# Hybrid RWKV-7 block: the recurrence of four head pairs side by side, memory products ahead, the last gates after them

## The chip, the cores and the metric

The kernel runs on one core of one Trainium2 chip, as a single program. The metric is device time in microseconds of one execution, as the median of several; a profile is one further execution with the hardware profiler on. Engines are named as in the profile: PE (TensorE, products; PEld its weight loads), DVE (VectorE), ACT (ScalarE), POOL (GpSimd), SP (SyncE, which issues nearly all DMAs here).

## The reference, cut to what matters

One layer of a decoder with two parallel token mixers over 1024 positions of width 1024, then cross-attention to 256 memory tokens and a feed-forward of width 4096, all in float32.

```python
h = rms_norm(x, norm_mix)
p = h @ w_in                     # r, k, v, w/a/g-down | conv B, C, x | gate A | gate B
out_a = rwkv7_branch(...)        # 8 heads of 64; the state recurrence below
#   S_t = S_{t-1} diag(w_t) + (S_{t-1} a_t) b_t^T + v_t k_t^T ;  y_t = S_t r_t
#   y = layer_norm per head (y) + sum(r * k * r_k) * v      (the bonus)
out_b = short_conv_branch(cb, cc, cx, conv_w)              # B * conv3(C * x)
merged = sigmoid(ga + bg_a) * (out_a @ w_proj_a) + sigmoid(gb + bg_b) * (out_b @ w_proj_b)
x = x + merged @ w_out_mix
x = x + memory_cross_attention(rms_norm(x), rms_norm(mem), w_q, w_kv, w_xo)
x = x + relu(rms_norm(x) @ w_up)**2 @ w_down
return rms_norm(x)
```

## The kernel before

**Large products.** Each float32 product is made of three: both operands are split into a rounded high part and a low part, and high x high, high x low and low x high are accumulated in one PSUM bank. ACT makes the high part of a weight block and DVE the low part (`w_splits`, L515); raw weights of 512 KB come through two buffers `wr` (`w_loads`, L428, in the order of `wlist`). Tokens are in two blocks of 512 columns. A projection job (one block of 128 output columns, `gemm`, L822) is 2 x 8 x 3 = 48 products of 512 columns.

**The recurrence.** The 8 heads are 4 pairs `j`; a pair in one block `b` of 512 tokens is a *window*, with 8 chunks of 64 tokens. For each window `wkv_prepare` (L1267) loads r, k, v and the decays, forms the scaled operands T1 and BK, then the bonus (L1340), the values SV (L1358, through a PSUM bank and four DVE copies, L1370), the chunk products of BK with T1 (L1400) and the transposes of BK. `wkv_invert` (L1429) solves the triangular system of every chunk on POOL, in 31 steps, with round trips through HBM. `wkv_chain` (L1486) then runs the chunks of two windows together: products of T1 with the state SV, of SV with T1 for the output Y and of an identity with SV; a copy on ACT; products with the inverse XT and with QZ; four evacuations by ACT and DVE in turn, into SV; products with BKt; four evacuations into the next chunk's SV. All of these are small float32 products of 64 columns. `wkv_out` (L1554) normalizes Y and adds the bonus.

**The order of the work.** A planner written in the kernel (`Scheduler`, L42) fixes the order of every engine's instructions when the program is built. It keeps a clock for each engine from costs of its own (L68 to L119), and each stream of work is a generator that yields the time at which it may go on. `need(tile)` (L202) is the time at which a tile will have been written, plus 0.7 us; a write counts 0.21 us after its end for other engines (L168). The side streams (preparations, inversions, recurrence, loads) go first whenever their time has come, otherwise the main stream emits one more large product (`run`, L227). At run time nothing but the semaphores holds an engine up, and each engine takes its instructions in the order that was written. In `wkv_chain` the margins on `need` are +0.2 us (L1506, L1531).

Windows go in the order (pair, block) of `ORDER` (L1589); preparations come one after the other, inversions as well, and recurrences by twos. `held` and `LIVE_P` (L288, L1597) bound the SBUF tiles in use, `take_s` (L1253) the two PSUM banks `s`.

**Main stream.** `main` (L2111) runs the 43 projection jobs `PROJ` (L601; the last 16 are the gates gb and ga), then 8 jobs for the keys of the memory (`mem_k`, L1651, 24 products of 256 columns each), 4 for its values (`mem_v`, L1668, 256 columns), then 8 `merge` jobs (L1729) that need all outputs of the recurrence, and then the rest of the layer. Weights of the memory products are loaded up to four ahead (L431, L411). `mem_prep` (L1620) normalizes and transposes the memory tokens; `gate_loads` (L1717) brings the gates back from HBM for the merge, and begins when the projection jobs are over and the last recurrence is done. The evacuation of a "cc" job (L1204) scales by the square of the norm, held in a tile `Rq`; `lora_side` (L1111) writes its results through store buffers `st`.

Of the kernel before, what the change touches and what calls it, by code (L numbers as in the profile page):

```python
# [17 lines left out]
P = 128  # L18
D = 1024
# [242 lines left out]
def tile_hybrid_block(  # L262
# [130 lines left out]
    def w_wide(w, k0, c0):  # L393
        return [(w[k0:k0 + 512, c0:c0 + 256].rearrange("(k p) n -> p k n", p=P), 0, 4)], [P, 4, 256]
# [15 lines left out]
    def w_raw(i):  # L410
        n = 2 if i in quads else 1  # L411
        more = i >= first_quad and (i - first_quad) % 2 if i in quads else (i > first_quad or i in light) and i % 4 > 1
# [102 lines left out]
    def w_splits():  # L515
        for i in range(2, len(wlist)):
# [36 lines left out]
            parts = 4 if i - 1 in light or i in light else 1  # L553
# [52 lines left out]
    wlist += [w_cols(win, job_off(k, i), n=32 if (k, i) == ("gd", 1) else P) for k, i in PROJ]  # L606
    MIX = [("k", i) for i in range(8)] + [("v", i) for i in range(4)] + [("m", i) for i in range(8)]
    for k, n in MIX:
        if k != "m":
            light.update(range(len(wlist), len(wlist) + (2 if k == "v" else 1)))  # L610
        if k == "k":
            wlist.append(w_cols(w_kv[0], n * P))
        elif k == "v":
            wlist += [w_wide(w_kv[0], kh * 512, D + n * 256) for kh in range(2)]
        else:
            wlist.append(w_pair(w_proj_b[0], w_proj_a[0], n * P))
# [493 lines left out]

    def lora_side(name, parts, b, dst, fin):  # L1111
        yield until(("x", 1))
        for j in range(4):
# [41 lines left out]
    def proj_stream(t, b, o):  # L1155
# [48 lines left out]
        elif kind == "cc":  # L1204
            if "Rq" not in prevs:
                prevs["Rq"] = hold([P, NB, TB])
                for q in range(NB):
                    ACT.activation(prevs["Rq"][:, q], Rt[:, q], AF.Square)
            yield need(prevs["Rq"])
            z = sb("st", [P, TB])  # L1210
            DVE.tensor_tensor(z[:], o[:], prevs["Rq"][:, b], op=ALU.mult)
            yield need(z)
            prevs["cc", i, b] = z
            done.add(("cc", i, b))
        elif kind == "cx":
            if (i, b) == (3, 1):
                drop(1)
# [31 lines left out]
    open_s = {"n": 0}  # L1249
# [3 lines left out]
    def take_s():  # L1253

        yield lambda: open_s["n"] < BUFS["s"]
        open_s["n"] += 1
# [10 lines left out]
    def wkv_prepare(w):  # L1267
# [72 lines left out]
        POOL.tensor_tensor(ta, ta, k, op=ALU.mult)  # L1340
        yield max(pace("DVE"), need(ta_))
        DVE.scalar_tensor_tensor(sq, r, vc("rk", j), ta, op0=ALU.mult, op1=ALU.mult)
        bs = sb("P", [P, 2, TB], F32R)
        yield need(tm_, bs)
        split(bs[:, 0], bs[:, 1], sq)
        yield need(bs) + LATE
        yield from take_s()
        o = ps("s", [P, TB])
        yield need(o)
        mm(o[:], cv["bdo"][:], bs[:, 0], True, False)  # L1350
        mm(o[:], cv["bdo"][:], bs[:, 1], False, True)
        yield max(pace("DVE"), need(o))
        DVE.tensor_tensor(sw, o[:], v, op=ALU.mult)
        give_s()
        dma(d_bv[cs, blk(b)], sw, ("bv", j, b))


        SV = sb("P", [P, NCH, 2, C])  # L1358
        w["SV"] = SV
        yield from take_s()  # L1360
        o = ps("s", [P, 4, 2, C])
        yield need(o) + LATE
        for q in range(4):
            mm(o[:, q], v[:, q * P:(q + 1) * P], cv["cmat"][:].rearrange("p h k -> p (h k)"))
        yield need(o)
        for h in range(2):
            O = HALF[1 - h]
            for par in range(2):
                yield pace("DVE")
                DVE.tensor_copy(SV[O, par:NCH:2, h, :], o[HALF[par], :, h, :])  # L1370
        give_s()


        nt_ = sb("P", [P, TB])
        NT, QZ, XT = c3(nt_[:]), c3(v), c3(sw)
        w["vs"], w["NT"], w["QZ"], w["XT"] = vs_, NT, QZ, XT

        def evac_products(o, q, h):
# [7 lines left out]
            yield pace("DVE")  # L1386
            DVE.tensor_tensor(QZ[H, c4, :], o[H, :, C:2 * C], rows(msk[H, C:2 * C], 4), op=ALU.mult)
            give_s()

        for q in range(2):  # L1390
            yield need(T1[0], T1[1], BK) + 2 * LATE
            os_ = []
            for h in range(2):
                yield from take_s()
                o = ps("s", [P, 4, 2 * C])
                yield need(o) + LATE
                os_.append(o)
# [17 lines left out]
        w["BKt"] = BKt  # L1415

# [12 lines left out]
    def wkv_invert(w):  # L1429

        NT, XT, Lb = w["NT"], w["XT"], w["Lb"]
        zz = sb("ex", [P, 2, 8, 32])
# [18 lines left out]
        for g in range(4):  # L1451
            SP.dma_start(dz[:, :, g, :], Z[32 * g:32 * g + 32])
        for h in range(2):
# [4 lines left out]
        yield need(w["vs"])  # L1458
# [27 lines left out]
    def wkv_chain(ws):  # L1486

        b = ws[0]["b"]  # L1490
        HW = [(h, HALF[h], i, w) for i, w in enumerate(ws) for h in range(2)]
        for h, H, i, w in HW:
# [4 lines left out]
        Y = [ps(t, [P, NCH, C]) for t in "yc"]  # L1497
        yield need(*Y)
# [3 lines left out]

        for c in range(NCH):
# [6 lines left out]
            yield need(o)  # L1510
            for h, H, i, w in HW:
                acc_mm(w["T1"][h][:, c, 0:C], w["SV"][:, c, h, :], o[H, 0, i], i == 0, True)
            for h, H, i, w in HW:
                acc_mm(w["SV"][:, c, h, :], w["T1"][h][:, c, C:2 * C], Y[i][H, c], c == 0)
            if keep:
                for h, H, i, w in HW:
                    acc_mm(ident[:, H], w["SV"][:, c, h, :], o[H, 2, i], False)
            ws_ = sb("s2", [P, 2, C])
            ACT.activation(ws_[:], o[:, 0], AF.Copy)
            yield need(ws_)  # L1520
            for h, H, i, w in HW:
                acc_mm(w["XT"][H, c, :], ws_[H, i], o[H, 1, i], False, True)
            if c:
                for h, H, i, w in HW:
                    acc_mm(w["SV"][H, c - 1, h, :], w["QZ"][H, c - 1, :], Y[i][H, c - 1], False, True)
            for h, H, i, w in HW:
                if h == 0:
                    ACT.activation(w["SV"][H, c, h, :], o[H, 1, i], AF.Copy, scale=w["d2"][H, c:c + 1])
                else:
                    DVE.tensor_scalar(w["SV"][H, c, h, :], o[H, 1, i], w["d2"][H, c:c + 1], None, op0=ALU.mult)  # L1530
            yield need(*[w["SV"] for w in ws]) + 0.2  # L1531
            if keep:
                if last:
                    for w in ws:
                        state[w["j"]] = const([P, C], f"state{w['j']}")
                for h, H, i, w in HW:
                    acc_mm(w["BKt"][:, c, h, :], w["SV"][:, c, h, :], o[H, 2, i], False, True)
# [643 lines left out]
```

## Time and profile before

| | us |
|---|---|
| median of 3 runs (lowest, highest) | 1795.97 (1790.7, 1798.21) |
| profiled execution | 1803.41 |
| its span, first to last instruction | 1801.7 |
| PE busy | 1745.5 |
| DVE busy | 1081.4 |
| ACT busy | 698.2 |
| POOL busy | 519.6 |

The mean granted TensorE clock of this execution was 0.989. The profile names instructions by the tiles they write and read: `psc<-s,P` is a product into a bank `c` from tile `s`. All operations pass through one helper, so the line is L256 everywhere and one goes by tiles: `psg` are banks of the large products, `psc` and `psy` those of the recurrence, `pss` those of preparations and other side work; `wr`, `wh`, `wl` are raw, high and low weights. A row of the timeline has start, duration, engine, operation and count; in square brackets stands the idle time before it and what ended it. A row of the windows has the stretch, the busy time and count of PE, PEld, DVE, ACT and POOL, the granted clock (PEclk), the DMA share and GB/s. A row of the waits has who waited for whom: us in total, times, longest.

### The profile page before, as it was taken

What the parts mean: (1) busy time and instruction counts of PE and PEld (TensorE: products, weight loads), DVE (VectorE), ACT (ScalarE), POOL (GpSimd) and SP (SyncE); (2) the same over time, 40 slices, a digit from 0 to 9 for tenths busy, and PEclk for the clock granted to TensorE, in tenths of its full rate; (3) what the DMA queues carried; (4) which work ended last, traced back from release to release, by engine and by line L of the source; (5) the groups of instructions that cost most, each with busy time, mean ns of one, the idle gap of its engine ahead of it and who ended that gap; (6) DMA issues with size and microseconds to landing.
All of it is one profiled execution on the core that took longest, in us unless ns stands there. A gap on an engine that the chain in (4) does not pass through costs nothing. (4 is left out here: it accounts for less than half of the span.)

```text
span 1801.7 us, 26657 instructions
## 1 busy us (share of the span) xinstructions
PE 1745.5 (97%) x9914; PEld 1423.6 (79%) x9914; DVE 1081.4 (60%) x1694; ACT 698.2 (39%) x1233; POOL 519.6 (29%) x872
## 2 busy tenths in 40 slices
PE   7899999999999999999999999999999999999998
PEld 5687777877877778988888877778888887888887
DVE  4478666666665334555647666597776775645543
ACT  5524323123233434422324434364444454534532
POOL 3017643744653201001413334342322310000000
PEclk9999999999999999999999999999999999999999
DMA  6543532332433526645745667235545479755441
GB/s 211 203 125 96 163 109 74 91 101 68 129 112 107 175 89 228 210 152 191 243 143 160 207 203 253 97 114 169 176 157 170 135 244 339 251 207 192 152 125 51
DMA packets 303360, 289.19 MB, mean 161 GB/s; under 512 B 40745, under 2 KB 223135, under 8 KB 303231
## 3 DMA queue, kind: packets, MB, share of 16 engines
q1 hardware_dynamic: 302158, 286.97, 49.5%
q8 instruction: 78, 1.28, 0.3%
q10 hardware_dynamic: 1072, 0.53, 0.1%
q14 instruction: 52, 0.42, 0.1%
HBM read 193.06 MB, written 94.37 MB: 160 GB/s over the span
## 5 line engine op out<-in xcount | busy, mean ns | idle before, releaser
L256 PE MATMUL psg<-H,wh 128*128 128x512 f32 x1808 | 583.2, 400 | 1.0 <-ACT H L256 1.0
L256 PEld LDWEIGHTS psg<-H,wh 128*128 128x128 f32 x1808 | 338.9, 190 | 72.2 <-ACT H L256 1.4
L256 PE MATMUL psg<-P,wh 128*128 128x512 f32 (+1 forms) x1240 | 370.5, 380 | 2.7 <-DVE P L256 2.7
L256 PE MATMUL psg<-H,wl 128*128 128x512 f32 x888 | 356.6, 402 | 0.0
L256 PEld LDWEIGHTS psg<-P,wh 128*128 128x128 f32 x1240 | 228.0, 188 | 46.6 <-DVE P L256 4.4
L256 PE MATMUL psg<-P,wl 128*128 128x512 f32 (+1 forms) x620 | 235.4, 380 | 1.5 <-DVE wl L256 1.5
L256 ACT ACTIVATE wh<-wr 128x1024 fp32r<-128x1024 f32 (+2 forms) x155 | 127.1, 839 | 209.4 <-PE psg L256 143.1
L256 PEld LDWEIGHTS psg<-H,wl 128*128 128x128 f32 x888 | 168.7, 190 | 34.9 <-DVE wl L256 0.3
L256 DVE TENSOR_TENSOR wl<-wr,wh 128x1024 fp32r<-128x1024 f32 (+2 forms) x146 | 149.6, 1040 | 62.0 <-ACT wh L256 61.1
L256 ACT ACTIVATE P<-P 128x512 fp32r<-128x512 f32 (+3 forms) x246 | 148.1, 634 | 91.2 <-DVE P L256 55.6
L256 DVE TENSOR_TENSOR P<-P,P 128x512 fp32r<-128x512 f32 (+2 forms) x204 | 152.3, 782 | 14.1 <-ACT P L256 12.7
L256 POOL TENSOR_TENSOR sm<-sm,mhalf 128x8 f32<-128x8 f32 (+2 forms) x18 | 22.5, 1252 | 443.5 <-DVE sm L256 443.5
L256 PEld LDWEIGHTS psg<-P,wl 128*128 128x128 f32 x620 | 116.7, 188 | 22.7 <-DVE wl L256 1.9
L256 POOL TENSOR_TENSOR ex<-ex,P 128x60 f32<-128x60 f32 (+24 forms) x248 | 98.2, 396 | 101.3 <-DMA P<-dn 85.8
L256 POOL TENSOR_TENSOR ex<-ex 128x60 f32<-128x60 f32 (+24 forms) x248 | 95.7, 386 | 19.4
L256 PE MATMUL pss<-P,wh 128*128 128x512 f32 x304 | 93.9, 390 | 0.0
L256 DVE TENSOR_SCALAR P<-psc,sm 64x64 f32<-64x64 f32 x120 | 34.9, 291 | 83.7 <-ACT P L256 79.4
L256 ACT ACTIVATE P<-psc,sm 64x64 f32<-64x64 f32 (+1 forms) x128 | 42.4, 332 | 98.4 <-PE psc L256 54.8
L256 DVE TENSOR_TENSOR P<-psg,P 128x512 f32<-128x512 f32 x44 | 30.3, 689 | 78.4 <-PE psg L256 63.6
L256 PE MATMUL psc<-P,P 128*64 128x64 f32 (+2 forms) x816 | 65.0, 244 | 9.0 <-ACT st L256 7.9
L256 PEld LDWEIGHTS psc<-P,P 128*64 128x64 f32 (+2 forms) x816 | 44.8, 141 | 34.5 <-issue 11.6
L256 PE MATMUL psc<-P,wh 128*128 128x512 f32 x216 | 67.1, 391 | 1.7 <-DVE P L256 1.7
(698 smaller groups left out, 2837.3 us busy)
## 6 DMA issues: line engine op xcount, KB each, us to landing
P<-d_t SPq DMA_DIRECT2D x56, 512.0 KB
wr<-in_w_in_dram SPq DMA_DIRECT2D x40, 512.0 KB
d_t<-P SPq DMA_DIRECT2D x64, 256.0 KB
d_x<-P SPq DMA_DIRECT2D x48, 256.0 KB
P<-d_x SPq DMA_DIRECT2D x24, 512.0 KB
d_t<-st SPq DMA_DIRECT2D x48, 256.0 KB
d_tg<-st SPq DMA_DIRECT2D x32, 256.0 KB
P<-d_tg SPq DMA_DIRECT2D x16, 512.0 KB
```

Source lines behind the costliest of these rows:

```text
L256: return fn(*args, **kw)
```

## The change

- **Recurrence.** Windows go block by block, and `wkv_chain` takes the four pairs of a block together, with two banks `c` (two windows in each) per chunk and Y in a bank for two chunks, copied out every second chunk. Margins on `need` fall from +0.2 to -0.4 us (-0.1 for the first half of T1), the copies of T1's result come before Y and ident, and each of the steps with XT and BKt is done half by half.
- **Preparation.** The chunk products come right after the operands; bonus and values are a stream of their own. A window's preparation and inversion are one stream, and the next preparation begins when this one's operands are there; POOL's part of the inversion is still one window at a time.
- **Memory and gates.** Memory keys and values come before the last five gate jobs; the values are two jobs of 512 columns. Their weights keep to the two raw buffers. `mem_prep` takes one half of the memory tokens at a time.
- **Others.** Lora results go to held tiles. A "cc" job multiplies by the norm twice, the second time on POOL. `merge_loads` waits for the memory.

`finish(c)` does the products with QZ of the four windows and, after every second chunk, copies Y out, on ACT, one copy per window. The diff, cut to its core:

```diff
     def w_wide(w, k0, c0):
-        return [(w[k0:k0 + 512, c0:c0 + 256].rearrange("(k p) n -> p k n", p=P), 0, 4)], [P, 4, 256]
+        return [(w[k0:k0 + 256, c0:c0 + 512].rearrange("(k p) n -> p k n", p=P), 0, 2)], [P, 2, 512]
...
-                yield lambda: i < ws["split"] + (4 if i in light and "proj" in done else 2)
+                yield lambda: i < ws["split"] + 2
...
+    HEAD = len(PROJ) - 5
+    wlist += wcols[:HEAD]
+    wlist += [w_cols(w_kv[0], n * P) for n in range(KD)]
+    wlist += [w_wide(w_kv[0], kq * 256, D + n * 512) for n in range(2) for kq in range(4)]
+    light.update(range(HEAD, len(wlist)))
+    wlist += wcols[HEAD:]
...
-            z = sb("st", [P, TB])
-            fin(z, o2, j)
-            dma(dst[cs, blk(b)], z[:], (name, j, b))
+            if j % 2 == 0:
+                zt = hold([P, 2, TB])
+            z = zt[:, j % 2]
+            fin(z, o2, j)
+            dma(dst[cs, blk(b)], z, (name, j, b))
...
-            DVE.tensor_tensor(z[:], o[:], prevs["Rq"][:, b], op=ALU.mult)
+            DVE.tensor_tensor(z[:], o[:], Rt[:, b], op=ALU.mult)
             yield need(z)
+            POOL.tensor_tensor(z[:], z[:], Rt[:, b], op=ALU.mult)
...
@@ wkv_prepare, ahead of the chunk products @@
+        sch.spawn(bonus_and_values(w, rk_, vs_, ta_, tm_))
+        done.add(("front", j, b))
...
@@ the bonus and the values, the same lines moved @@
+    def bonus_and_values(w, rk_, vs_, ta_, tm_):
...
@@ wkv_invert @@
+        yield lambda: not open_s["inv"]
+        open_s["inv"] = True
...
         for c in range(NCH):
             last = c == NCH - 1
             keep = not last or b == 0
-            yield need(*[w["SV"] for w in ws]) + 0.2
-            o = ps("c", [P, 3, 2, C])
+            o2 = [ps("c", [P, 3, 2, C]) for _ in range(2)]
+            if c % 2 == 0:
+                Y[c // 2] = ps("yg"[c // 2 % 2], [P, 4, 2, C])
+                yield need(Y[c // 2])
+            for q in range(2):
+                yield need(o2[q], *[w["SV"] for w in ws[2 * q:2 * q + 2]]) - (0.4 if q else 0.1)
+                for h, H, i, w in PART[q]:
+                    acc_mm(w["T1"][h][:, c, 0:C], w["SV"][:, c, h, :], o2[q][H, 0, i % 2], i % 2 == 0, True)
+            wq = []
+            for q in range(2):
+                wq.append(sb("s2", [P, 2, C]))
+                if q:
+                    DVE.tensor_copy(wq[q][:], o2[q][:, 0])
+                else:
+                    ACT.activation(wq[q][:], o2[q][:, 0], AF.Copy)
...
+            for q in range(2):
+                yield need(wq[q]) - 0.4
+                for h, H, i, w in PART[q]:
+                    acc_mm(w["XT"][H, c, :], wq[q][H, i % 2], o2[q][H, 1, i % 2], False, True)
+                for h, H, i, w in PART[q]:
+                    u, d = w["SV"][H, c, h, :], w["d2"][H, c:c + 1]
+                    if h == 0:
+                        ACT.activation(u, o2[q][H, 1, i % 2], AF.Copy, scale=d)
+                    else:
+                        DVE.tensor_scalar(u, o2[q][H, 1, i % 2], d, None, op0=ALU.mult)
             if c:
+                finish(c - 1)
...
+            for q in range(2):
+                yield need(*[w["SV"] for w in ws[2 * q:2 * q + 2]]) - 0.4
+                for h, H, i, w in PART[q]:
+                    acc_mm(w["BKt"][:, c, h, :], w["SV"][:, c, h, :], o2[q][H, 2, i % 2], False, True)
...
-    ORDER = [(0, 0), (1, 0), (0, 1), (1, 1), (2, 0), (3, 0), (2, 1), (3, 1)]
+    ORDER = [(j, b) for b in range(NB) for j in range(4)]
...
+            sch.spawn(wkv_window(i))
+            yield until(("front", j, b))
...
+    def wkv_window(i):
+        yield from wkv_prepare(windows[i])
+        done.add(("prep", i))
+        yield from wkv_invert(windows[i])
+        drop(2)
+        done.add(("win", i))
...
@@ mem_prep @@
+        for m in range(2):
+            for h in range(2):
+                junk = sb("st", [P, TB])
+                ACT.activation(junk[:], mt[:, h * TB:(h + 1) * TB], AF.Square, accum_out=ss[:, h:h + 1])
...
-        yield from gemm(PROJ, hh, hl, proj_evac, key="h", scale="r1", pair=2)
+        yield from gemm(PROJ[:HEAD], hh, hl, proj_evac, key="h", scale="r1", pair=2)
+        for n in range(KD):
+            yield from mem_k(n)
+        for n in range(2):
+            yield from mem_v(n)
+        yield from gemm(PROJ[HEAD:], hh, hl, proj_evac, scale="r1")
         done.add("proj")
```

More of the change, by code (lines that the diff above doesn't have):

```diff
@@ L1337, in wkv_prepare @@
         w["d2"] = d2
[L1340 to L1376, printed above, removed]
+        QZ, XT, NT = c3(r), c3(k), c3(cum)
+        w["rk"], w["NT"], w["QZ"], w["XT"] = rk_, NT, QZ, XT
+        sch.spawn(bonus_and_values(w, rk_, vs_, ta_, tm_))
+        done.add(("front", j, b))
         def evac_products(o, q, h):
@@ L1415, in wkv_prepare @@
         w["BKt"] = BKt
+        yield until(("val", j, b))
+    def bonus_and_values(w, rk_, vs_, ta_, tm_):
+        j, b = w["j"], w["b"]
+        r, k, v, sw, ta = rk_[:, 0, :], rk_[:, 1, :], vs_[:, 0, :], vs_[:, 1, :], ta_[:, 0, :]
+        POOL.tensor_tensor(ta, ta, k, op=ALU.mult)
+        yield max(pace("DVE"), need(ta_))
+        sq = tm_[:, 0, :]
+        DVE.scalar_tensor_tensor(sq, r, vc("rk", j), ta, op0=ALU.mult, op1=ALU.mult)
+        done.add(("bs", j, b))
+        bs = sb("P", [P, 2, TB], F32R)
+        yield need(tm_, bs)
+        split(bs[:, 0], bs[:, 1], sq)
+        yield need(bs) + LATE
+        yield from take_s()
+        o = ps("s", [P, TB])
+        yield need(o)
+        mm(o[:], cv["bdo"][:], bs[:, 0], True, False)
+        mm(o[:], cv["bdo"][:], bs[:, 1], False, True)
+        yield max(pace("DVE"), need(o))
+        DVE.tensor_tensor(sw, o[:], v, op=ALU.mult)
+        give_s()
+        dma(d_bv[j * P:(j + 1) * P, blk(b)], sw, ("bv", j, b))
+        SV = w["SV"] = sb("P", [P, NCH, 2, C])
+        yield from take_s()
+        o = ps("s", [P, 4, 2, C])
+        yield need(o) + LATE
+        for q in range(4):
+            mm(o[:, q], v[:, q * P:(q + 1) * P], cv["cmat"][:].rearrange("p h k -> p (h k)"))
+        yield need(o)
+        for h in range(2):
+            O = HALF[1 - h]
+            for par in range(2):
+                yield pace("DVE")
+                DVE.tensor_copy(SV[O, par:NCH:2, h, :], o[HALF[par], :, h, :])
+        give_s()
+        done.add(("val", j, b))
     def wkv_relayout(w):
@@ L1526, in wkv_chain @@
[L1526 to L1534, printed above, removed]
-                        state[w["j"]] = const([P, C], f"state{w['j']}")
-                for h, H, i, w in HW:
-                    acc_mm(w["BKt"][:, c, h, :], w["SV"][:, c, h, :], o[H, 2, i], False, True)
-                for h, H, i, w in HW:
+                    acc_mm(ident[:, H], w["SV"][:, c, h, :], o2[i // 2][H, 2, i % 2], False)
@@ L1611, in wkv_chains @@
         drop(3)
-        for i in range(0, len(ORDER), 2):
-            yield until(("win", i), ("win", i + 1))
-            yield from wkv_chain([windows[i], windows[i + 1]])
-            done.update((("chain", i), ("chain", i + 1)))
-    mk = {}
+        for b in range(NB):
+            ids = range(4 * b, 4 * b + 4)
+            yield until(*[("win", i) for i in ids])
+            yield from wkv_chain([windows[i] for i in ids])
+            done.update(("chain", i) for i in ids)
     def mem_prep():
-        yield until(("ml", "b"))
-        yield lambda: held["n"] + 7 <= LIVE_P
-        held["n"] += 7
+        yield until(("prep", 7))
@@ L1648, in mem_prep @@
-        drop(3)
+            mt = sb("P", [P, D])
+            SP.dma_start(mt[:], mem[0, m * P:(m + 1) * P, :])
+            ss = sb("sm", [P, 8])
+            yield need(mt)
+            for h in range(2):
+                junk = sb("st", [P, TB])
+                ACT.activation(junk[:], mt[:, h * TB:(h + 1) * TB], AF.Square, accum_out=ss[:, h:h + 1])
+            yield need(ss)
+            DVE.tensor_tensor(ss[:, 2:3], ss[:, 0:1], ss[:, 1:2], op=ALU.add)
+            r = rstd_of(ss[:, 2:3], 1, 1.0 / D, RMS_EPS)
@@ new lines, in mem_prep @@
+            yield need(r)
+            ACT.activation(mt[:], mt[:], AF.Copy, scale=r[:, 0:1])
+            ms = slice(m * P, (m + 1) * P)
+            for q in range(2):
+                yield need(mt)
+                yield from take_s()
+                o = ps("s", [P, 4, P])
+                yield need(o)
+                for k in range(4):
+                    PE.transpose(o[:, k], mt[:, (4 * q + k) * P:(4 * q + k + 1) * P], ident[:])
+                yield need(o)
+                for k in range(4):
+                    gained(mh[q][:, k, ms], ml[q][:, k, ms], o[:, k], vc("nmem", 4 * q + k))
+                give_s()
@@ L1668, in mem_v @@
     def mem_v(n):
-        mh, ml = mk["h"], mk["l"]
-        o = [ps("g", [P, 256]) for _ in range(2)]
-        for kh in range(2):
+        o = [ps("g", [P, TB]) for _ in range(2)]
+        for kq in range(4):
             w_ = []
```

145 lines of the change are left out of this document (56 added, 89 removed).

## The prediction

> **What bounds the kernel now.** I read the page first, its busy table and the chain that ended last.
>
> ```profile
> span 1801.7 us, 26657 instructions
> PE 1745.5 (97%) x9914; PEld 1423.6 (79%) x9914; DVE 1081.4 (60%) x1694; ACT 698.2 (39%) x1233; POOL 519.6 (29%) x872
> PE 37%; DVE 1%; issue 1%; DMA 1%; ACT 0%; SPq 0%; DVEq 0%; POOLq 0%; POOL 0%; ACTq 0%
> ```
>
> TensorE is busy for 97% of the span and is all but alone on the last chain, so a microsecond counts only if PE's own stream loses it. That stream is written out by the planner: PE takes its instructions in that order, and what can shrink is the work itself, the changes between large and small products, and waits at semaphores. The chain of waits, cut to the stretch from 1500 to 1600, gives the price of a large product where nothing disturbs it; the grouped lines, cut to 250 to 690, give the recurrence.
>
> ```profile
> 1524.28 21.76 PE pss L256 x96
> ```
>
> ```profile
> L256 PE MATMUL psc<-P,P 128*64 128x64 f32 x624 | 35.5, 231 | 1.1 <-DVE P L256 1.1
> L256 PE MATMUL psc<-s,P 64*64 64x64 f32 x256 | 14.3, 230 | 0.0
> L256 PE MATMUL psc<-P,ident 128*64 128x64 f32 x240 | 12.2, 222 | 0.0
> ```
>
> A 512-column product takes 21.76/96 = 0.227 us. The products with XT (tile s) are 8 instructions per chunk of a pair of windows, so 256 are 32 chunk runs; ident goes with the 30 runs that keep a state. A run visits small products three times (T1, Y and ident; then XT and QZ; then BKt): 32 + 32 + 30 = 94 visits. Their idle time is 1.1 us in all: the order written by hand asks for each operand late enough. The price of a visit is in PE's timeline:
>
> ```profile
> 271.90 0.40 PE L256 MATMUL psg<-H,wl 128*128 128x512 f32 x1
> 272.23 0.45 PE L256 MATMUL psc<-P,P 128*64 128x64 f32 x8
> 272.51 0.29 PE L256 MATMUL psy<-P,P 128*64 128x64 f32 x4
> 272.63 0.29 PE L256 MATMUL psc<-P,P 128*64 128x64 f32 x4
> ...
> 273.08 0.73 PE L256 MATMUL psg<-H,wh 128*128 128x512 f32 x2
> 273.65 0.40 PE L256 MATMUL psg<-H,wl 128*128 128x512 f32 x1
> ...
> 274.26 0.28 PE L256 MATMUL psy<-P,P 64*64 64x64 f32 x4
> 274.38 0.28 PE L256 MATMUL psc<-P,P 64*64 64x64 f32 x4
> ```
>
> Four small instructions take 0.12 us (272.51 to 272.63), 0.03 each. The large one before the visit takes 0.33 instead of 0.227 (+0.10), the 24 small ones 0.85 instead of 0.70 (+0.15), the two after it 0.57 instead of 0.45 (+0.12). So a visit costs 0.36 us beside its products, and 94 cost 34 us. A change of shape inside a visit costs as well:
>
> ```profile
> 304.15 0.45 PE L256 MATMUL psc<-P,P 128*64 128x64 f32 x8
> 304.53 0.33 PE L256 MATMUL psy<-P,P 64*64 64x64 f32 x4
> ```
>
> Eight instructions took 0.38 instead of 0.24: 0.14 us.
>
> **The change part by part.** The sum is against the profiled execution, 1803.4 us (its span and 1.7 us around it); the median of the runs is 1796.0, and I carry the difference over to it.
>
> 1. *Visits.* The recurrence keeps its products and goes from 32 runs of two windows to 16 runs of four. T1, Y, ident, XT and QZ may now follow each other, since the copies of T1's result lie under Y and ident; BKt of either half comes apart. That is 16 + 15 + 15 = 46 visits; I take 53, since some copies will come late and large products be put between. 41 fewer at 0.36 are -14.8 us; 16 changes of shape inside the long visit at 0.14 are +2.2. Bounds: 46 visits (-15.1 net) to 94 (0).
>
> 2. *The gates.* This is the price of it. The margin after which a step's operands are asked for falls from +0.2 to -0.4 us (-0.1 for T1's first half). The timelines of ScalarE and VectorE after the XT products of one run:
>
> ```profile
> 274.53 0.31 ACT L256 ACTIVATE P<-psc,sm 64x64 f32<-64x64 f32 x1 [1.06 <-PE psc L256]
> 275.20 0.31 ACT L256 ACTIVATE P<-psc,sm 64x64 f32<-64x64 f32 x1 [0.36 <-DVE P L256]
> ```
>
> ```profile
> 274.88 0.29 DVE L256 TENSOR_SCALAR P<-psc,sm 64x64 f32<-64x64 f32 x1 [0.85 <-ACT P L256]
> 275.54 0.29 DVE L256 TENSOR_SCALAR P<-psc,sm 64x64 f32<-64x64 f32 x1 [0.38 <-ACT P L256]
> ```
>
> The four evacuations of a bank don't run side by side: each waits for the other engine's. They end at 275.83, 1.57 us after the last XT product (274.26); with a step to PE, 1.6. The planner lets the two engines overlap: by its costs (L72 to L83, L168) it has the operands 1.05 us after the products, and adds 0.7 (`need`) and the margin: 1.95 before, so no wait, 1.35 now. Worked through for one run: BKt's first half reaches PE at about 1.5 us and waits 0.1; the second half's four evacuations share both engines, end a microsecond after the first's, and BKt waits 0.2 there; T1 of the next chunk waits 0 and 0.3 at its halves. In chunks 2, 4 and 6 four copies of Y stand on ScalarE ahead of the state's evacuations:
>
> ```profile
> L256 ACT ACTIVATE s<-psc 128x128 f32<-128x128 f32 x32 | 8.9, 277 | 52.8 <-PE psc L256 52.8
> L256 DVE TENSOR_TENSOR wl<-wr,wh 128x1024 fp32r<-128x1024 f32 x26 | 33.2, 1278 | 6.9 <-ACT wh L256 6.4
> ```
>
> The first row is a copy of the same 128x128 form: four are 1.1 us, and T1 then waits 0.6 and 0.7. So 0.6 us without Y and 1.6 with; 1.0 on the mean, 15 us. All later large products on PE are queued behind each wait. Bounds: 1 us (gates as quiet as before) to 40 (a weight split of the second row, 1.28 us, ahead of a group in most runs). Visits and gates together: +1.3 after taking off the 1.1 that was there.
>
> [...]
>
> 3. *Bonus and values beside the products, own memory preparation, lora results in tiles of their own.* PE's waits between 100 and 750 us:
>
> ```profile
> PE pss L256 <- DVE P L256: 5.5, 8, 1.7
> PE pss L256 <- ACT P L256: 5.0, 5, 3.0
> PE psc L256 <- ACT st L256: 1.7, 1, 1.7
> PE psg L256 <- DVE wl L256: 1.5, 2, 1.3
> ```
>
> In the first row the products of T1 with BK wait for a bank that VectorE's copies of the values still hold (L1370 runs right ahead of L1400). With the values in a stream of their own those copies are no longer just ahead: -4, between -5.5 and +3, since the same banks and VectorE serve both. The second row is the memory's transposes, behind a norm whose power runs on GpSimd; now each half has its own norm and ScalarE works on 512 columns: -3, between -5 and +2. The third is the lora's ScalarE behind a store buffer: -0.9, half of it.
>
> 4. *The clock.* Three stretches with little work on PE are followed by a lower granted clock (column PEclk):
>
> ```profile
> 308.00:318.60 10.60, 10.12 (x70) 8.22 (x70) 1.27 (x4) 2.13 (x5) 5.84 (x15) 0.68 0.26 80
> 376.40:380.00 3.60, 3.60 (x39) 2.96 (x37) 2.19 (x5) 0.00 (x0) 2.02 (x8) 0.53 0.35 63
> 606.00:612.00 6.00, 4.75 (x17) 3.58 (x17) 2.10 (x3) 4.03 (x6) 0.30 (x2) 0.72 0.25 58
> ```
>
> They lost 10.6 x 0.32 + 3.6 x 0.47 + 6.0 x 0.28 = 6.8 us. The last follows the memory's wait of part 3. With those waits shorter I take two thirds as gone, -4.5, between -6.8 and +3 (four outputs now come together).
>
> 5. *Memory products ahead, gates last.* The memory's values become 96 products of 512 columns instead of 192 of 256.
>
> ```profile
> 700.13 0.40 PE L256 MATMUL psg<-P,wh 128*128 128x256 f32 x2
> ...
> 700.49 0.28 PE L256 MATMUL psg<-P,wh 128*128 128x256 f32 x1
> ```
>
> Three take 0.36, so 192 x 0.12 = 23.0 against 96 x 0.227 = 21.8: -1.2. Their 16 weight loads go past five gate jobs on SP's queue and keep two raw buffers, not four.
>
> ```profile
> 706.59 0.42 SPq L256 DMA_DIRECT2D P<-d_tg  x1
> 708.25 0.38 SPq L256 DMA_DIRECT2D wr<-in_w_kv_dram  x1
> ```
>
> ```profile
> 712.18 0.72 ACT L256 ACTIVATE wh<-wr 128x256 fp32r<-128x256 f32 x2
> ```
>
> A load is split 3.9 us after its issue; with the split's 1.5 a buffer turns in about 5.4, two give a weight per 2.7 us, and PE uses one in 24 x 0.12 = 2.9. That just holds: +2, between -1.5 (the fourth wait above gone) and +8. The loads for the merge gates, issued from 706.59 on, now start as the merge starts; three banks give 36 x 0.227 = 8.2 us of products before PE needs an evacuation, so 0, or 3 if a load takes twice 3.9. The convolution's extra GpSimd product has 48 large products of cover (10.9 us): 0. The other stores keep their number.
>
> ```profile
> 675.83 0.28 PE L256 MATMUL psc<-P,P 64*64 64x64 f32 x4
> 747.81 0.63 PE L256 MATMUL psg<-P,wh 128*128 128x512 f32 x2
> ```
>
> The last recurrence product (675.83) came 72 us before the first merge product (747.81). Two longer chains start later, but windows now overlap up to the inversion; I cost the order of the windows at 0, the 72 us being the cover.
>
> **Sum:** +1.3 - 4 - 3 - 0.9 - 4.5 - 1.2 + 2 = -10.3 us: 1793 for a profiled execution, 1786 for the median.
>
> **The rivals.** *Gates quiet* (A): the evacuations run side by side as the planner has them, or large products happen to fill. Part 2 is then 0 and the sum -25: 1771. For it speaks that before only 1.1 us were lost in 94 visits; against it the alternation above. *The gates become the bound* (B, slower): in the chunks, PE waits at all four gates because VectorE's splits (1.28 us) and evacuations stand ahead of a group whose two engines already take turns. At 3 us per run, part 2 is 45 instead of 15: +20, 1816. It decides from 1.65 us per run on, where the -10 is used up. For it: VectorE is in use 60% of the span; against: the planner counts those splits. *Clock* (C, slower): a long visit with its waits leaves PE so idle that the granted clock falls, as at 376.4. One such stretch is 3.6 x 0.47 = 1.7 us; in each of 16 runs 27 us: 1813. [...] *Nothing comes of it* (D): large products are put between all small ones again, and parts 3 and 4 only move: 1796.
>
> **How the numbers follow.** Forecast 0.45, A 0.15, B 0.16, C 0.06, D 0.18. A measurement of this kernel can tell about 0.5%, 9 us, from no change. A and two thirds of the forecast's spread lie beyond that: 0.45 faster; B, C and a little of the forecast are slower: 0.24; the rest, 0.31, is the same. The range runs from 1767, a little beyond A, to 1813, which takes in C and leaves out the upper half of B.
>
> **What would show it.** In the new profile: the visits per chunk run (3 to 4 in PE's timeline); the wait of PE's psc products for DVE and ACT tiles (about 15 us in place of 1.1); the first two rows of part 3 smaller; fewer stretches of low clock between 300 and 620; the gap before wl in the memory products; the last recurrence product still ahead of the merge. Psc waits above 25 us, or a recurrence that ends after the gate jobs, would make the prediction wrong.

## The result, and the profile after

| | before | after |
|---|---|---|
| median, us (lowest, highest) | 1795.7 (1790.7, 1805.5) | 1816.9 (1813.3, 1823.8) |
| profiled execution, us | 1803.4 | 1814.5 |
| mean granted clock | 0.989 | 0.984 |

After takes 1.0114 of the time of before (95%: 1.0085 to 1.0143): 21 us slower, where 10 us faster was forecast. The page's opening, its busy table and its chain, for after:

```profile
span 1812.8 us, 26502 instructions
PE 1743.0 (96%) x9818; PEld 1431.0 (79%) x9818; DVE 1086.2 (60%) x1705; ACT 689.1 (38%) x1231; POOL 521.7 (29%) x881
PE 36%; DVE 1%; issue 1%; DMA 1%; ACT 0%; SPq 0%; DVEq 0%; POOLq 0%; POOL 0%; ACTq 0%
```

PE is still the bound and has 96 instructions fewer, but is idle for more of a longer span. PE's waits of after between 100 and 760 us:

```profile
PE pss L256 <- DVE P L256: 13.9, 11, 4.6
PE psc L256 <- DVE P L256: 11.9, 29, 1.2
PE psc L256 <- DVE s L256: 4.4, 4, 1.5
PE psg L256 <- ACT wh L256: 2.1, 2, 1.9
PE psg L256 <- ACT st L256: 1.9, 1, 1.9
PE pss L256 <- ACT P L256: 1.8, 2, 1.2
PE psc L256 <- ACT s L256: 1.1, 3, 0.5
PE psg L256 <- DVE wl L256: 1.0, 1, 1.0
```

The recurrence's gates (the three psc rows) cost 17.4 us, as forecast (15). The first row, 5.5 before and forecast to shrink, is 13.9. The windows of after, with the granted clock in the third column from the right:

```profile
100.00:200.00 100.00, 93.86 (x517) 76.05 (x516) 63.97 (x111) 33.39 (x52) 52.32 (x147) 0.97 0.41 122
200.00:300.00 100.00, 97.42 (x570) 79.45 (x569) 70.16 (x113) 21.11 (x30) 62.90 (x153) 0.98 0.40 108
300.00:400.00 100.00, 90.35 (x1078) 69.77 (x1076) 52.56 (x118) 30.57 (x95) 24.40 (x55) 0.98 0.18 48
400.00:500.00 100.00, 94.73 (x569) 76.79 (x569) 73.59 (x127) 23.73 (x42) 60.61 (x120) 0.97 0.45 136
500.00:600.00 100.00, 97.36 (x592) 78.82 (x590) 50.64 (x97) 34.62 (x65) 62.44 (x182) 1.00 0.42 119
600.00:700.00 100.00, 85.33 (x1099) 72.52 (x1100) 50.55 (x143) 45.97 (x146) 6.67 (x4) 0.93 0.38 115
700.00:770.00 70.00, 69.76 (x302) 56.99 (x301) 24.82 (x36) 23.55 (x36) 10.35 (x8) 0.98 0.69 204
```

The shortfall of a window is its length times what the clock lacks to 1.00: 3 + 2 + 2 + 3 + 0 + 7 + 1.4 = 18.4 us in all. Of the same windows of before two lie under 1.00, which makes 7 us:

```profile
300.00:400.00 100.00, 96.91 (x697) 76.83 (x695) 59.49 (x108) 23.36 (x44) 51.51 (x121) 0.95 0.39 106
600.00:700.00 100.00, 96.31 (x774) 73.19 (x773) 37.99 (x81) 40.09 (x85) 12.49 (x13) 0.98 0.40 124
```

So the clock took 11 us, where it was to give 4.5. Where the largest wait comes from is seen at 160 us. PE's timeline, the products of T1 with BK:

```profile
160.50 0.48 PE L256 MATMUL pss<-P,P 64*128 64x128 f32 x2
165.61 2.04 PE L256 MATMUL pss<-P,P 64*128 64x128 f32 x14 [4.62 <-DVE P L256]
```

and VectorE's in the same stretch, with the four copies of the values out of their bank:

```profile
160.63 0.86 DVE L256 COPY P<-pss 64x256 f32<-64x256 f32 x2
...
163.57 0.41 DVE L256 COPY P<-pss 64x256 f32<-64x256 f32 x1
163.90 0.67 DVE L256 TENSOR_TENSOR P<-st,P 32x512 fp32r<-32x512 f32 x1
164.60 0.42 DVE L256 CAST P<-P 32x512 fp32r<-32x512 f32 x1
165.03 0.43 DVE L256 COPY P<-pss 64x256 f32<-64x256 f32 x1
```

The copies are let in one at a time between VectorE's other work, and the last ends at 165.46; PE goes on at 165.61, and everything behind these products on PE waits along. The 14 products are those of the second half of the window (4 of its 8 chunks). In the changed kernel the values take one of the two banks `s` between the two halves. The second half asks for both banks (`take_s(2)`), and the values' bank is given back (`give_s`) when the last copy has been written into VectorE's order. So the second half is written behind the copies, as the chunk products were in before. Five such waits of these products add up to 9.7 of the 13.9 us; in before four of them make 3.8, and a fifth, which the profile puts down to POOL, 1.4. VectorE has the evacuations of the first half among its work just ahead (154.10 to 159.74); that this is why the copies come later is argued, not shown. Such a wait is no mark of the new stream alone: in e10 below, which has the preparation of before, the same products waited 3.67 us behind a copy:

```profile
161.79 1.13 PE L256 MATMUL pss<-P,P 64*128 64x128 f32 x14 [3.67 <-DVE P L256]
```

One run of the recurrence, in PE's timeline of after (Y stands in `psg` and `psy` in turn):

```profile
355.35 0.45 PE L256 MATMUL psc<-P,P 128*64 128x64 f32 x8 [0.42 <-DVE P L256]
355.61 0.67 PE L256 MATMUL psg<-P,P 128*64 128x64 f32 x16
356.07 0.43 PE L256 MATMUL psc<-P,ident 128*64 128x64 f32 x8
357.74 0.62 PE L256 MATMUL psc<-P,ident 128*64 128x64 f32 x8 [1.24 <-DVE s L256]
358.29 1.12 PE L256 MATMUL psc<-s,P 64*64 64x64 f32 x16
359.20 1.06 PE L256 MATMUL psy<-P,P 64*64 64x64 f32 x16
```

T1, Y, ident, XT and QZ follow each other without a large product. Counted so, after has 51 visits in all (53 forecast), before 96: 45 x 0.36 = 16 us saved at the prediction's price, which no run measures by itself. The memory's evacuation row (pss for ACT) fell from 5.0 to 1.8, as forecast. The first merge product came at 765.01 instead of 747.81.

Against before: visits -16.2 and +2.2 for shapes, gates +16.3, values +8.4, memory preparation -3.2, weights and stores +1.8, values by 512 columns -1.2, clock +11.4. That is +19.5 of the 21; the visits, the shapes and the values by 512 columns stand in it at the prediction's prices. It says where the time went, not why.

### The profile page after: what moved, and what is told of

It reads as the page before. It is cut to its first block, busy times and chain, and to the rows that moved or that the text cites. A ratio compares the mean times of both kernels' runs of the same rounds, so it can differ in the third digit from the quotient of the medians.

```text
span 1812.8 us, 26502 instructions
## 1 busy us (share of the span) xinstructions
PE 1743.0 (96%) x9818; PEld 1431.0 (79%) x9818; DVE 1086.2 (60%) x1705; ACT 689.1 (38%) x1231; POOL 521.7 (29%) x881
## 5 line engine op out<-in xcount | busy, mean ns | idle before, releaser
L256 PE MATMUL psg<-P,wh 128*128 128x512 f32 (+1 forms) x1240 | 376.3, 383 | 2.7 <-DVE P L256 2.7
L256 PE MATMUL psg<-H,wl 128*128 128x512 f32 x888 | 352.7, 397 | 0.0
L256 ACT ACTIVATE wh<-wr 128x1024 fp32r<-128x1024 f32 (+2 forms) x171 | 136.1, 819 | 249.6 <-PE psg L256 158.8
L256 DVE TENSOR_TENSOR wl<-wr,wh 128x1024 fp32r<-128x1024 f32 (+2 forms) x162 | 163.1, 1021 | 59.1 <-ACT wh L256 58.0
L256 POOL TENSOR_TENSOR sm<-sm,mhalf 128x8 f32<-128x8 f32 (+3 forms) x19 | 23.0, 1219 | 490.9 <-DVE sm L256 490.9
L256 POOL TENSOR_TENSOR ex<-ex,P 128x60 f32<-128x60 f32 (+24 forms) x248 | 89.9, 363 | 35.5 <-DMA P<-dn 19.8
L256 PEld LDWEIGHTS pss<-P,wh 128*128 128x128 f32 x304 | 57.1, 188 | 12.4 <-DVE P L256 0.5
L256 ACT ACTIVATE P<-P,vec 128x512 f32<-128x512 f32 (+2 forms) x57 | 40.5, 710 | 67.9 <-DVE P L256 57.3
L256 DVE TENSOR_TENSOR st<-psg,P 128x512 f32<-128x512 f32 x40 | 27.5, 688 | 59.6 <-PE psg L256 58.7
```

The lines of the kernel that those rows point to most:

```text
L256: return fn(*args, **kw)
```

## The experiments

Ratios are against before, measured beside each run; medians in us. **Theory**: the bank wait of the values and the half clock behind waits cost it, the four-wide recurrence is neutral. **Rivals**: the gates; the memory stage; the outputs that come together; the order of the windows.

**e1, bonus and values in line again.**

```diff
-        sch.spawn(bonus_and_values(w, rk_, vs_, ta_, tm_))
+        yield from bonus_and_values(w, rk_, vs_, ta_, tm_)
```

> Undoes one part: bonus and values run inside the preparation again, ahead of the chunk products; all else as changed. Theory (waits at several places, each followed by a stretch at half clock): the waits of pss products for VectorE fall from 13.9 us to about 6, the half-clock stretches at 163 and 272 us go with them, so about 13 us less than the changed kernel: 1804. Rival (the loss sits in the memory stage): these waits only move, 1817.

1810.6, 1.0081 (1.0061 to 1.0102). PE's waits of e1 between 100 and 800 us:

```profile
PE psc L256 <- DVE P L256: 13.1, 33, 0.8
PE pss L256 <- ACT P L256: 13.0, 3, 11.2
PE pss L256 <- DVE P L256: 5.9, 11, 1.3
```

The wait for the values fell to 5.9 and the clock from 100 to 400 us was 1.00, but a wait of 11.2 us came up that after didn't have. PE's timeline there:

```profile
595.99 1.97 PE L256 MATMUL pss<-ident,P 128*128 128x128 f32 x8 [11.20 <-ACT P L256]
```

PE had come to the end of the projections that stand ahead of the memory products, and the second half of the memory tokens wasn't there. The time fell by 6, where 13 were expected.

**e2, one engine for each bank's evacuations** (both places in the recurrence).

```diff
-                    if h == 0:
+                    if q == 0:
```

> In the changed kernel, the four evacuations of a bank all go to one engine: ScalarE for the first two windows, VectorE for the other two, so that no evacuation waits for the other engine's. If the taking of turns sets the gates, the recurrence's waits fall from 17 us to about 6, 11 us less: 1806. If VectorE's other work ahead of the evacuations sets them, they stay at 15 us or more and the time stays near 1817.

1809.5, 1.0072 (1.0053 to 1.0091): -7. The psc waits fell to 7.6 for ACT P, 1.9 for DVE P and 2.2 for s, 11.7 in all. So the alternation costs about 6 us of the 17.

**e3, memory products after all projections.**

```diff
-    HEAD = len(PROJ) - 5
+    HEAD = len(PROJ)
```

> In the changed kernel, the memory products come after all projection jobs again, with weights up to four ahead; the recurrence is unchanged. Rival (the loss sits in the memory stage, where the second recurrence lies over the memory products): nearly all of it comes back, about 1797. Theory (waits at several places): only the memory's waits (4.9 to 1.5 us) and the half-clock stretches at 668, 689 and 699 us go, about 11 us less: 1806.

1805.0, 1.0049 (1.0030 to 1.0067): -12, as the theory had it, but not by its half-clock stretches: the shortfall of the clock was 19 us against 18 in after. What fell were PE's waits, from 40 to 32 us in all; the pss wait for the values stayed at 13.9.

**e4, the four outputs one after the other.**

```diff
-        for w in ws:
-            sch.spawn(wkv_out(w, ...))
+        def outs():
+            for w in ws:
+                yield from wkv_out(w, ...)
+        sch.spawn(outs())
```

> In the changed kernel, the outputs of the four windows come one after the other instead of all at once; the work is the same. If the half-clock stretches at 409 and 668 us follow the 32 nearly empty products (128x2) that the four outputs issue together, both go: about 5 us less, 1812. If they follow the waits in the recurrence, they stay: 1817.

1827.7, 1.0174 (1.0155 to 1.0193): 11 slower. The waits for pss rose to 22.0 (DVE) and 7.7 (ACT), and the shortfall of the clock over the seven windows from 18 to 26 us. So the time is a miss. But the two stretches that were asked about did go: from 403.4 to 424 and from 660 to 690 e4 ran at 1.00, where after had 0.83 and 0.87. The lower clock came at other places: e4 had 0.95 from 300 to 400, 0.90 from 600 to 700 and 0.95 from 700 to 770, after 0.98, 0.93 and 0.98.

**e5 and e6, e1 with e3, and both with e2.**

> In the changed kernel both at once: bonus and values inside the preparation, and the memory products after all projection jobs with weights four ahead. What stays of the change is the recurrence by fours with its narrow margins and the order of the windows. Theory (losses at separate places add up): 6 and 12 us less than the changed kernel, 1799, with waits of pss products for VectorE near 6 us. If a wait taken away at one place comes back at another: about 1805, no better than either part alone.

> The same with the evacuations of a bank on one engine each. Theory (adds up): the recurrence's waits fall from about 15 us to 8, 7 us less, 1792, a little under the kernel before. If the waits move: 1800 or more.

e5: 1815.3, 1.0109 (1.0088 to 1.0131); e6: 1809.8, 1.0076 (1.0059 to 1.0094). The gains don't add: e5 is slower than e3, and by its median than e1. In e6 PE reaches the merge at 734.0, 31 us before after did, and stops there. Its largest wait:

```profile
PE psg L256 <- ACT P L256: 20.0, 2, 10.8
```

The merge's second operand needs the outputs of all four pairs. SP issued the eight loads of them (`sh<-d_y`) from 711.85 to 759.54, one per 6 us or so, each behind the multiplication of the last. They stand behind the loads of the first operand (`sh<-d_ob`), which needs nothing from the recurrence. Two of those eight rows in SP's timeline of e6, one after the other:

```profile
611.36 0.86 SPq L256 DMA_DIRECT2D sh<-d_ob  x1
675.99 0.42 SPq L256 DMA_DIRECT2D sh<-d_ob  x1
```

For 65 us none was issued, until the last recurrence product (664.05) and the first store of an output of block 1 (675.62) were past; in e17 all eight went from 568.82 to 603.79. The condition ahead of these loads in the kernel (`merge_loads`) is the limit on SBUF tiles in use (`held`, `LIVE_P`), and a wide run keeps five tiles of each of its four windows until their outputs are stored (`drop(5)`). That this limit is what held them is read from the kernel; no run lifted it.

**e7 and e8, the margins**: the old ones in after, and the new ones in before.

```diff
-yield need(...) - 0.4
+yield need(...) + 0.2
```

> In the changed kernel, the margins of the recurrence are wide again: +0.2 us for the operands of T1, of BKt and of the last QZ (0 for those of XT). Theory (narrow margins trade visits for waits): the recurrence's waits fall from 17 us to below 3, visits rise from 51 to about 85, 34 x 0.36 = 12 us; the two nearly cancel, 1812 to 1818. Rival (the waits also halve the clock, so they cost more than their length): 1808 or less, with less time at half clock between 340 and 670 us.

> The kernel before with the changed kernel's narrow margins in its recurrence by pairs: -0.1 us for T1, -0.4 for XT and BKt. Theory (the planner counts four evacuations as done 0.5 us too early): waits of psc products rise from 1.1 us to some 0.4 us at two gates of each of 32 runs, 25 us, visits fall by 20 at most (7 us), so 1805 to 1815. Rival (pairs have slack enough): no wait above 5 us, 1797 or less.

e7: 1810.0, 1.0077 (1.0058 to 1.0097), 62 visits, psc waits 12: -7, between theory and rival. From 340 to 670 us the clock was 0.98 in both, so the rival's reason fails. e8: 1796.1, 0.9994 (0.9976 to 1.0012): the two-wide recurrence doesn't feel the margins.

**e9, e1 and e2 with both loads of the memory tokens issued together.**

```diff
+        mts = [sb("P", [P, D]) for _ in range(2)]
         for m in range(2):
-            mt = sb("P", [P, D])
-            SP.dma_start(mt[:], mem[0, m * P:(m + 1) * P, :])
+            SP.dma_start(mts[m][:], mem[0, m * P:(m + 1) * P, :])
```

> After with three edits together, the last gates kept where they are: bonus and values in line again (alone -6, with a new wait of 11.2 us in the memory preparation), evacuations of the first two windows all on ACT and of the other two all on DVE (alone -7.4), and the two loads of the memory tokens issued together, so that the second doesn't stand behind later work in SP's queue. If the losses are separate places of PE's stream, they add: 1817 - 6 - 7 - 11 = 1793 (1788 to 1799), with the first merge product near 745 us, PE's pss waits under 8 and psc waits under 13 us. Rival (a loss that is taken away at one place comes back at the next, as when the memory products stood last): 1803 to 1810, with a wait of PE's psg products for ACT or DVE near the merge of 8 us or more, or half clock there.

1826.0, 1.0162 (1.0141 to 1.0183): worse than after, and outside both ranges. SP's queue in e9:

```profile
572.24 5.93 SPq L256 DMA_DIRECT2D d_tg<-st  x2
584.10 0.38 SPq L256 DMA_DIRECT2D wr<-in_w_kv_dram  x1
584.58 0.53 SPq L256 DMA_DIRECT2D d_tg<-st  x1
585.16 2.60 SPq L256 DMA_DIRECT2D dz<-ex  x4
589.83 1.80 SPq L256 DMA_DIRECT2D P<-dz  x4
591.68 0.92 SPq L256 DMA_DIRECT2D P<-in_mem_dram  x2
```

and PE:

```profile
592.11 0.28 PE L256 MATMUL pss<-P,P 32*32 32x32 f32 x2 [10.38 <-issue]
```

A load of memory weights that waits 6.1 us for a raw buffer (SP's longest wait for wl) holds the queue to 584.10; the round trip of an inversion (dz, then P from dz) and the memory tokens stand behind it, and PE, out of projections, for 10.4 us. (The profile names no releaser for that wait; that it is the round trip is read from the order of the rows.) In e1 the second load of the memory tokens had been issued at 587.0, 12 us after the first. So the wait moved from one side stream to another at the same place.

**e10, all of the change but the recurrence, the preparation and the order.** The functions `wkv_prepare` to `wkv_chain`, `ORDER` and what starts them are those of before.

> Before with all of the change but the recurrence, the preparation and the order of the windows: memory preparation by halves, memory products ahead of the last five gates, values by 512 columns, lora results in held tiles, the norm applied twice. Theory (the loss sits in the recurrence, the stream of its own for bonus and values, and the order of the windows): these parts give about what the prediction gave them, -3 -1.2 -0.9 +2, so 1793 (1788 to 1798), PE's psc waits stay at 1 to 3 us and the first merge product comes at 743 to 748 us. Rival (the memory products ahead of the gates are what costs): 1804 or more, with waits for wl, wh or st in the memory products over 5 us.

1789.7, 0.9950 (0.9933 to 0.9967): 8 faster than before. Memory ahead and gates last are no cost there. The row of the values was 9.5 us in it (5.5 in before) and the psc waits 6.4, yet the shortfall of the clock was 5 us.

**e11, after with the two-wide recurrence of before.**

```diff
-            yield from wkv_chain([windows[i] for i in ids])
+            for i in ids[::2]:
+                yield from wkv_chain([windows[i], windows[i + 1]])
```

> After with the recurrence of before: runs of two windows, margins +0.2, one bank each, but everything else of the change, the windows block by block and the last four outputs in two lots of two. Visits back to 94 (+16 us against after), waits at the gates back to about 1 (-18). Theory (the four-wide recurrence is neutral in sum; the loss is in the bank wait of bonus and values, the clock and the order): 1812 (1807 to 1818), pss waits for DVE still over 10 us. Rival (the four-wide recurrence is what costs, by its waits and the lower clock behind them): 1800 or less.

1812.0, 1.0077 (1.0049 to 1.0104): as the theory had it. So 22 us lie between e10 and e11, in the preparation or the order.

**e12 and e13, one of the two put back in e11**: the order of before (`ORDER`), or bonus and values in line (the diff of e1).

> The kernel of e11 (all of the change but the four-wide recurrence, 1812) with the windows in the order of before, (pair 0 and 1, then 2 and 3). Theory (most of the 22 us between e10 and e11 is the preparation: a stream of its own for bonus and values, the next preparation begun early, and the half clock behind its bank waits): 1806 (1801 to 1812), pss waits for DVE still 10 us or more, half clock between 100 and 400 us again. Rival (the order block by block is most of it, since all outputs of block 1 then come at the end): 1796 or less.

> The kernel of e11 (windows block by block) with bonus and values in line ahead of the chunk products. Theory (preparation): pss waits for DVE fall from 14.2 to about 7 and half-clock stretches before 400 us go, so 1812 - 8 - 4 = 1800 (1796 to 1805). Rival (order): 1808 or more.

e12: 1808.1, 1.0051 (1.0032 to 1.0070), not to be told from e11. e13: 1785.0, 0.9926 (0.9902 to 0.9949). One line is worth 27 us beside two-wide runs, twice what was expected. PE's waits of e11:

```profile
PE pss L256 <- DVE P L256: 14.2, 10, 4.0
PE psg L256 <- DVE wl L256: 6.0, 4, 2.0
PE pss L256 <- issue: 3.5, 3, 1.8
```

and of e13:

```profile
PE psc L256 <- DVE P L256: 6.6, 7, 4.2
PE pss L256 <- DVE P L256: 4.7, 8, 1.0
```

Values -9.5, weights -6, issue -2.8, psc +3, and -2.5 in the smaller rows together: PE's waits fall from 33 to 16 us. The shortfall of the clock over the same seven windows is 17 us in e11 and 5 in e13, -12. Together that is about 30; the two profiled spans differ by 28.

**e14 and e15, four-wide in block 0 alone, values in line**; e15 with e2's evacuations.

```diff
+            step = 2 if b else 4
-            yield from wkv_chain([windows[i] for i in ids])
+            for i in ids[::step]:
+                yield from (wkv_chain2 if b else wkv_chain)([windows[k] for k in range(i, i + step)])
```

> After with bonus and values in line, block 0 by the four-wide recurrence and block 1 by two runs of two windows as before. Theory (what the four-wide recurrence costs is its place: in block 1 nothing of it can start before the eighth inversion, at about 600 us, so PE runs out of projections ahead of the gates, then the recurrence, the outputs and the loads of the merge stand in a row behind it): half of the visits stay saved (-7), half of the gate waits stay (+5), the wait of 11.2 us of e1 is gone and the first merge product comes near 733: 1784 (1779 to 1790). Rival (the four-wide runs themselves cost, by their waits and the clock behind them): half of the 26 us between e13 and e1 stays, 1798 (1794 to 1804), with psc waits of 10 us and half clock at block 0's run.

> The kernel of e14, and in the four-wide run of block 0 the evacuations of the first two windows all on ACT and of the other two all on DVE. Theory: the alternation of the two engines costs half of the 7.4 us of e2, since half of the runs are left: 1780 (1775 to 1786). Rival (large products of the stream fill or the wait moves): no change against e14 within 2 us.

e14: 1804.5, 1.0046 (1.0022 to 1.0070); e15: 1801.3, 1.0026 (1.0010 to 1.0042). Twenty above e13: my theory of block 1 alone fell. So did the rival's reason, since the window from 300 to 400, with block 0's run, stood at 1.00. e2's evacuations are worth 3 us here, within the intervals. The stretch from 600 to 700, in e14:

```profile
600.00:700.00 100.00, 86.30 (x783) 70.92 (x783) 52.54 (x122) 48.51 (x129) 14.29 (x10) 0.86 0.56 173
```

and in e13:

```profile
600.00:700.00 100.00, 92.87 (x778) 77.43 (x775) 47.91 (x105) 47.15 (x120) 14.39 (x10) 0.97 0.63 187
```

The wide run in block 0 starts at 343 us, when its fourth inversion is done, where the first two-wide one started at 241; and the last recurrence ends at 676 instead of 657.

**e16 and e17, e15 and e13 with the memory products after all projections** (the diff of e3).

> The kernel of e15 (four-wide in block 0, two-wide in block 1, bonus and values in line, one engine per bank) with the memory products after all projections. Theory (a wide run waits for the inversions of all its windows, so the later recurrence comes some 20 us later and is bunched between 600 and 700 us, where the memory products and few large ones are all that PE has to put beside it; what is lost there is waits and half clock): with the gate jobs to fill 600 to 700 us, PE is over 94 per cent busy there at a clock of 0.95 or more, the first merge product comes at 728 to 735, no long wait for the merge's operands since pairs 0 and 1 are out by 620: 1783 (1778 to 1790). Rival (a wide run costs by itself, wherever it stands): 1797 or more.

> The kernel of e13 (two-wide everywhere, in line; 1785) with the memory products after all projections: the control for e16. Theory: in e13 PE is 93 per cent busy between 600 and 700 us at 0.97, so there are only some 5 us to win, and the loads of the merge's operands come nearer to the merge: 1785 (1780 to 1791). Rival (memory products ahead of the gates are a gain in themselves): 1792 or more.

e16: 1789.6, 0.9955 (0.9940 to 0.9971); e17: 1780.2, 0.9918 (0.9893 to 0.9943). From 600 to 700 us PE was busy for 95.4 us in e16, at a clock of 0.98.

Filling that stretch is worth 12 us to the wide kernel. To the two-wide one it is worth 5 by the medians, which the intervals of e13 and e17 don't tell from nothing. So the bunching cost some 7 us or more. The other 9.5 between e16 and e17 stay with the wide run: 77 visits against 96 (-7), but psc waits 8.8 instead of 4.8, values 7.7 instead of 4.7, and a clock shortfall of 9 instead of 2 us.

e17 is the fastest by its median, and not to be told from e13: two-wide runs block by block, values in line, the change's memory preparation and wide memory values, and the memory products where before had them.

## Why the prediction was wrong

The two steps of the change that matter can be read side by side, by four kernels that are otherwise alike (medians, us):

| | values in line | values in a stream of their own |
|---|---|---|
| runs of two windows | 1785.0 (e13) | 1812.0 (e11) |
| runs of four windows | 1810.6 (e1) | 1816.9 (after) |

Either step alone costs 26 or 27 us, and the second then only 5 or 6 more. So no one step holds the loss: both have to be undone.

**Parts 1 and 2, visits and gates: right in their own rows, not in the whole.** 51 visits against 53, waits of 17.4 against 15. After against e11 is +5 us by the medians against +1.3 forecast, which the two intervals don't tell apart. But that agreement is luck of the place: with the values in line the same step costs 26 us (e1 against e13). In this kernel the two engines take turns at a bank: in the rows of before, four evacuations end 1.57 us after the last XT product. e2, in which no two engines share a bank's evacuations, gains 7 us, with psc waits of 11.7 us in place of 17.4. The rows show waits at the program's semaphores; whether the chip would let both engines in at once no run here shows.

**Part 3, the values: this step failed.** The prediction had it that "with the values in a stream of their own those copies are no longer just ahead: -4, between -5.5 and +3". The row went from 5.5 to 13.9. The copies are still just ahead: the second half of a window's chunk products is written behind them and waits for their bank. The line costs 27 us beside two-wide runs (e13 against e11), with what follows from it, and 6 beside four-wide ones (e1 against after).

**Part 4, the clock: failed, of the same cause.** -4.5 was taken because two waits were to vanish; one grew. The bound of +3 was far too near; measured +11. In e13 against e11 the one line takes 9.5 us of bank wait and 12 of clock with it. The link is no fixed rate: e10 had the same 9.5 us in that row and lost 5 us of clock.

**Part 3, memory preparation, and part 5: right in direction where nothing else was late.** The memory's row fell by 3.2, against 3 forecast; e10 makes the small parts together -8, against -3. But the order of the windows, "at 0, the 72 us being the cover", was right only for two-wide runs (e12, e13), and this step failed too. A four-wide run waits for four inversions, and in block 1 for all eight. In after this didn't show yet: the merge came 102 us behind the last recurrence product, and PE waited nowhere between 760 and 800. With the values in line and the memory products last, e6 stands 20 us at the merge: its last load for it is issued 95 us after the last recurrence product, and 72 had been counted. The two-wide e17 had issued four of the eight loads by 631, before the last recurrence was over. Beside after, e1 gains only 6, since PE then comes early to the memory preparation.

**The rivals.** The time was B's (1816) by luck, not by B's mechanism: 17.4 us in 16 runs is 1.1 us per run, under its point of decision of 1.65. Of C, 11 of its 27 us of clock came, but hardly in the long visits: the window from 300 to 400, which holds block 0's runs, is short by 2 us, and the runs of block 1 end at 663, ahead of most of the low stretches of that window (from 668 on).

**What stays open.** The 26 us between e1 and e13 are explained to 16 by rows: gates +9, the memory wait +12, clock +8, visits -13. That a wide run with all inversions early would gain was not tried, nor one with more tiles allowed, so that the merge's first loads don't wait for it. And each edit makes the planner write the whole order anew. e8 changed it and left the time where it was, while e9 came out 16 us slower than e1 and e2, which it contains: steps of 5 to 10 us here can be luck of the order, and only the large ones (27 and 26 us) stand clear of that.

## What to carry to other kernels

Before work is moved "beside" other work, look at what it holds while it waits: a bank held by copies that are let in one by one stops the engine whose next product needs it (4.62 us in after), whichever stream the copies belong to. Waits were paid again in part as clock here, where PE is the bound: between e11 and e13 18 us of waits went with 12 us of clock, so, as an estimate from these two, price a new wait at up to 1.7 times its length. Widening a run saves changes of shape but starts it when the last of its inputs is ready, and it keeps the buffers of all its windows meanwhile; count what is then left to put beside it, and the loads that start only after it. When two changes are made together, try all four combinations: here undoing either one alone showed 5 or 6 us of the 32.

## What the runs showed of the hardware

In after the granted clock fell to 0.50 behind a stretch in which PE shows as busy for 1.75 of 3.40 us, and behind one in which it shows as busy for all 3.40. Windows of after, cut to 3.4 and 6.8 us:

```profile
354.50:357.90 3.40, 1.75 (x44) 1.50 (x46) 2.71 (x5) 0.59 (x2) 2.51 (x3) 1.00 0.00 0
357.90:361.30 3.40, 3.40 (x49) 2.73 (x47) 1.08 (x5) 1.49 (x7) 0.00 (x0) 0.50 0.02 5
405.70:409.10 3.40, 3.40 (x26) 3.22 (x27) 1.21 (x5) 1.00 (x2) 2.35 (x2) 1.00 0.00 0
409.10:415.90 6.80, 6.80 (x32) 5.47 (x31) 1.41 (x5) 0.00 (x0) 4.32 (x3) 0.50 0.01 2
```

In the first row lie waits of 0.42 and 1.24 us (at 355.35 and 357.74, in the run shown above), and the next 3.4 us ran at 0.50. In the third PE shows as fully busy, but most of its 26 products were 128x2 ones of the outputs; 6.8 us at 0.50 followed. In e4, where these products of the four windows come apart, that stretch ran at 1.00; so the near-empty products are the likelier cause. It isn't settled: a wait of 1.18 us right before them in after was 0.48 us in e4.
